# mLSTM heads 0 to 2: norm factors through a DRAM round trip in place of two diagonals and two products with ones

## The chip, the cores and the metric

The kernel runs on one core of a Trainium2 chip. The metric is the device time of one execution in microseconds (us), lower is better; a measurement is the median of several runs. The engines of the core have their own instruction streams and meet through semaphores: PE (matrix products; PEld is its weight load), DVE (vector), ACT (activation functions), POOL (here: memsets and the issue of some transfers) and SP (issue of the other transfers). Each engine takes its instructions strictly in the order of its own stream: an instruction that waits holds up everything behind it on that engine.

## The reference

The program is a two-layer encoder trunk on 512 tokens of width 1024: an mLSTM layer with a memory cross-attention beside it, a gated MLP, a band-attention layer, a second MLP. The change lies in the mLSTM layer, where each of four heads (192 wide) ends in a normalisation per token:

```python
num = einsum('bhts,bhse->bhte', s, vv) + inter[..., None] * einsum('bhtd,bhde->bhte', qq, c_st)
den = sum(s, axis=-1) + inter * einsum('bhtd,bhd->bht', qq, n_st)
h = num / maximum(abs(den), exp(-m_t))[..., None]
...
hm = hm * rsqrt(mean(hm * hm, axis=-1, keepdims=True) + EPS)      # per token and head
hm = hm.reshape(bsz, seq, A_WIDTH) * a_head_g
mix_out = hm * sigmoid(o)
...
x = x + concatenate([mix_out, mem_out], axis=-1) @ w_out
```

## The kernel before, in words

Activations lie with channels on the 128 partitions and the 512 tokens along a row. Numbers are kept to full precision by splitting each operand into a high and a low part (`split`: an ACT cast `L134` and a DVE subtraction `L135`), so that one product becomes three matmuls (`mm3`, lines 178 to 180). A weight block goes DRAM, `wr` (load on SP), `wh` (ACT cast), `wl` (DVE subtraction), with three buffers of each.

An mLSTM head (`mlstm_head(h)`) is a generator. It makes the causal scores of four blocks of 128 keys, each shorter than the one before (512, 384, 256, 128 queries): a row of decay terms (two small matmuls at lines 1134 and 1135), its exponential on ACT (`L1137`), the score product (three matmuls and two at `L517`), their product on DVE (`L1143`), and the split into the `pt` tile. Then `products(s)` multiplies the values with the four blocks of `pt`; block 3, 128 wide, comes last. Squares of the sums (`L1170`) are added over channels by products with a small constant (`mcf`, lines 1177 and 1178), which gives a column: one number per token, with tokens on partitions, 128 x 4. From this column DVE computes the factor `fc` per token with some 12 tiny instructions (`L1182` to `L232`).

`fc` has tokens on partitions, but is needed along the row and on all partitions. Before, `diagonal` (lines 134, 135, 241) split it into two parts and wrote each as four diagonal 128 x 128 blocks, and `spread` (`L254`) multiplied each of the two by a matrix of ones on PE. The sum, in PSUM, has the 512 factors along the row of every partition. `L1191` multiplies it with the head's output `og` (twice: 128 channels, and 64 that share a tile with another head), and the split of that result makes `mixes`, the operand of the output projection.

What stands beside the heads: `weave(job, fill, each)` runs a head's generator and takes, for each of its yields, `each` (or `each` times the number yielded) steps of one `mm3` from a queue of independent work, the projections that make later heads' queries, keys and gates (`a_tiles`, `a_memory_queries`). Head 0 is woven with the remaining projections, head 1 follows when `og[2]` is there, then memory attention over heads 0 and 1, head 2, memory attention over heads 2 and 3, and head 3 with the output projection:

```python
fill = chain(a_tiles(2), a_memory_queries(0), a_tiles(3, 4), a_tiles(5), a_memory_queries(1))
weave(mlstm_head(0), fill, 1.4)
until(lambda: og[2] is not None, fill)
weave(mlstm_head(1), fill, 1.125)
...
weave(mlstm_head(2), fill, 1.417)
```

The written order is not the last word: outside the stretches marked `manual_schedule` a scheduler puts each engine's instructions into a new order by its own estimate of when their inputs are there. `pin` keeps POOL's transfers in the order of the program. Memory attention, which follows heads 1 and 2, begins with queries (`head_queries`: memsets on POOL at `L497`, ACT `L498` and `L501`, DVE `L499`), scores (`L517`), a maximum (`L571`, DVE), an exponential (`L574`, ACT), a reciprocal and a scaling (`L575`, `L577`, DVE) and transposes on PE (`L586`).

Of the kernel before, what the change touches and what calls it, by code (L numbers as in the profile page):

```python
# [9 lines left out]
F32 = mybir.dt.float32  # L10
# [6 lines left out]
P = 128  # L17
D = 1024
S = 512
# [4 lines left out]
AH = 4  # L24
# [22 lines left out]
def f(ap):  # L47
    return ap.bitcast(F32)
# [3 lines left out]
def trunk(  # L52
# [19 lines left out]
    V, A, G = nc.vector, nc.scalar, nc.gpsimd  # L72
# [8 lines left out]
    dram = ctx.enter_context(tc.tile_pool(name="dram", bufs=1, space=bass.MemoryType.DRAM))  # L81

    def sb(tag, shape, dtype=F32):
        count[0] += 1
        return pool.tile(shape, dtype, tag=tag, name=f"{tag}{count[0]}", bufs=bufs[tag])

    def ps(tag):
        count[0] += 1
        return psum.tile([P, S], F32, tag=tag, name=f"p{tag}{count[0]}", bufs=pbufs[tag])

    def small(n=4):
        return sb("s", [P, 32])[:, :n]
# [38 lines left out]
    pin = tc.keep_in_program_order  # L131

    def split(hi, lo, src, on_act=True, pinned=False):
        high = A.copy(hi, src) if on_act else V.tensor_copy(hi, src)  # L134
        low = V.tensor_tensor(out=lo, in0=src, in1=f(hi), op=ALU.subtract)  # L135
        if pinned:
            pin(high)
            pin(low)
# [37 lines left out]
    def mm3(o, lh, ll, rh, rl, first, last, more=False):  # L176

        nc.tensor.matmul(o, lh, rh, start=first, stop=False, skip_group_check=more)  # L178
        nc.tensor.matmul(o, lh, rl, start=False, stop=False, skip_group_check=more)  # L179
        nc.tensor.matmul(o, ll, rh, start=False, stop=last, skip_group_check=more)  # L180

    def project(w, c0, act, tag="mm", lo=None):


        n = len(act)
        src = rows(w, c0, P)
        wh, wl = weights(src, n, P) if lo is None else summed_weights(lo, src, n, P)
        o = ps(tag)
        for k in range(n):
            mm3(o, wh[:, k, :], wl[:, k, :], act[k][0], act[k][1], k == 0, k == n - 1)  # L190
            yield
        return o
# [30 lines left out]
    def rsqrt(y, v):  # L223
        n = v.shape[-1]
        yi = y.bitcast(I32)
        V.tensor_scalar(yi, v.bitcast(I32), 1, None, op0=ALU.logical_shift_right)
        V.tensor_scalar(yi, yi, -1, 0x5F3759DF, op0=ALU.mult, op1=ALU.add)
        t = small(n)
        for _ in range(3):
            V.tensor_mul(t, y, y)  # L230
            V.scalar_tensor_tensor(t, t, -0.5, v, op0=ALU.mult, op1=ALU.mult)
            V.scalar_tensor_tensor(y, t, 1.5, y, op0=ALU.add, op1=ALU.mult)  # L232

    def diagonal(c):

        cs = [sb("s", [P, 32], F32R)[:, :TT] for _ in range(2)]
        split(*cs, c, on_act=False)
        dgs = []
        for c in cs:
            dg = sb("t", [P, S], F32R)  # L240
            V.tensor_tensor(
                out=dg.rearrange("p (a b) -> p a b", a=TT),
                in0=ident.unsqueeze(1).to_broadcast([P, TT, P]),
                in1=f(c).unsqueeze(2).to_broadcast([P, TT, P]),
                op=ALU.mult,
            )
            dgs.append(dg)
        return dgs

    def spread(dgs, tag):  # L250

        o = ps(tag)
        for i, dg in enumerate(dgs):
            nc.tensor.matmul(o, onesr, dg, start=i == 0, stop=i == 1)  # L254
        return o
# [255 lines left out]
    def head_scores(o, h, q, tsl, k, c, first, keys_first=False):  # L511

        for i, part in enumerate(q):
            a, b = part[h][:, tsl], k[h][:, c]
            if keys_first:
                a, b = b, a
            nc.tensor.matmul(o, a, b, start=first and i == 0, stop=i == 1)  # L517
# [24 lines left out]
    def queries(o, row):  # L542

        if row is None:
            return head_queries(o, HD**-0.5)
        q = sb("t", [P, S])
        V.scalar_tensor_tensor(q, o, HD**-0.5, row, op0=ALU.mult, op1=ALU.mult)
        return head_queries(q)
# [571 lines left out]
    def a_memory_queries(hp):  # L1120
        memq[hp] = queries((yield from project(w_in, 4 * AW + 2 * AH + hp * P, act)), None)

    def mlstm_head(h):
        hp, odd = divmod(h, 2)
        sh = 3 * hp + 1
        full = 3 * hp + 2 * odd
        rs = slice(HD, P) if odd else slice(0, HD)
        pt = sb("pt", [P, 5 * S], F32R)

        def weighted_scores(s):  # L1130
            n = S - s * P
            sl = slice(s * P, (s + 1) * P)
            r = ps("sc")
            nc.tensor.matmul(r[:, :n], sels[s % 2][:, h, :], rp[s // 2][:, s * P :], start=True, stop=False)
            nc.tensor.matmul(r[:, :P], identr, maskr, start=False, stop=True)
            e = sb("t", [P, S])
            A.activation(e[:, :n], r[:, :n], AF.Exp, bias=acol[:, s, h : h + 1])  # L1137
            yield
            o = ps("sc")
            kf, qf = ks[full], qs[full]  # L1140
            mm3(o[:, :n], kf[0][:, sl], kf[1][:, sl], qf[0][:, s * P :], qf[1][:, s * P :], True, False)
            head_scores(o[:, :n], odd, qs[sh], slice(s * P, S), ks[sh], sl, False, True)
            V.scalar_tensor_tensor(e[:, :n], o[:, :n], DH**-0.5, e[:, :n], op0=ALU.mult, op1=ALU.mult)  # L1143
            split(pt[:, RO[s] : RO[s + 1]], pt[:, 1280 + RO[s] : 1280 + RO[s + 1]], e[:, :n])
            yield

        nums = []

        def products(s):
            if not nums:  # L1150
                nums.extend(ps("tr") for _ in range(2))
            for o, c in zip(nums, (3 * P, 2 * P) if odd else (0, P)):
                mm3(
                    o[:, s * P :], vh[hp][s][:, c : c + P], vl[hp][s][:, c : c + P],
                    pt[:, RO[s] : RO[s + 1]], pt[:, 1280 + RO[s] : 1280 + RO[s + 1]], s == 0, s == TT - 1,
                )
            yield

        yield from weighted_scores(0)
        yield from weighted_scores(1)  # L1160
        yield from weighted_scores(2)
        yield from products(0)
        yield from weighted_scores(3)
        yield from products(1)
        yield from products(2)
        yield from products(3)
        sqs = []
        for o, j, r in ((nums[0], full, slice(0, P)), (nums[1], sh, rs)):
            sq = sb("t", [P, S])
            A.activation(sq, o, AF.Square)  # L1170
            sqs.append(sq)
            V.tensor_tensor(out=og[j][r, :], in0=o[r, :], in1=og[j][r, :], op=ALU.mult)
        yield
        st = ps("sc")
        for T in range(TT):
            sl = slice(T * P, (T + 1) * P)
            nc.tensor.matmul(st[:, 2 * T : 2 * T + 2], sqs[0][:, sl], mcf[:, 0, :], start=True, stop=False)
            nc.tensor.matmul(st[:, 2 * T : 2 * T + 2], sqs[1][:, sl], mcf[:, 1 + odd, :], start=False, stop=True)
            yield 0.581
        st = st[:, : 2 * TT].rearrange("p (t c) -> p t c", c=2)  # L1180
        z, fc = small(), small()
        V.tensor_tensor(out=z, in0=st[:, :, 1], in1=floor2[:, :, h], op=ALU.max)  # L1182
        V.tensor_scalar(z, z, EPS, 1e-35, op0=ALU.mult, op1=ALU.max)
        V.scalar_tensor_tensor(z, st[:, :, 0], 1.0 / DH, z, op0=ALU.mult, op1=ALU.add)
        rsqrt(fc, z)
        dg = diagonal(fc)
        yield 2.673
        fb = spread(dg, "sc")
        yield
        for j, r in ((full, slice(0, P)), (sh, rs)):  # L1190
            V.tensor_tensor(out=og[j][r, :], in0=fb[r, :], in1=og[j][r, :], op=ALU.mult)  # L1191
            if mixes[j] is None:
                mixes[j] = sb("u", [P, S], F32R), sb("u", [P, S], F32R)
            split(mixes[j][0][r, :], mixes[j][1][r, :], og[j][r, :])
# [10 lines left out]
    fill = chain(a_tiles(2), a_memory_queries(0), a_tiles(3, 4), a_tiles(5), a_memory_queries(1))  # L1205
    memkv = load_memory_kv(0)
# [3 lines that stand above are left out]
    until(lambda: memq[0] is not None, fill)  # L1210
    weave(memory_attention(memq[0], memkv, 0, mixes), fill, 1.463, 4)
    until(lambda: og[4] is not None, fill)
    weave(mlstm_head(2), fill, 1.417)
    run(fill)
    reload_x()
# [285 lines left out]
```

## Time and profile before

| | before |
|---|---|
| three timed runs | 1211.79, 1211.98, 1214.2 us; median 1211.98 us |
| profiled execution, first to last instruction (span) | 1209.9 us |
| PE busy | 1196.0 us, 99% of the span |
| DVE, ACT, POOL busy | 945.1, 711.1, 125.3 us |
| granted PE clock | 0.999 |
| last step of `fc` in heads 0, 1, 2 (`L232`) | starts at 135.76, 159.55, 216.91 us |

The profiled execution is known by its span; the median of the timed runs is 2.1 us above it, which lies ahead of the first and behind the last instruction or in the spread between runs. The three heads of the change lie between 130 and 225 us of the span. A row of the timeline gives start, length, engine, line and operation; matmuls are pipelined, so what one costs is the distance to the next start, not its length.

### The profile page before, as it was taken

The numbers are of one execution on the slowest core, as the hardware profiler recorded it, in microseconds if no ns is written. First come the engines' busy times: TensorE is split into PE (matmuls) and PEld (weight loads), VectorE is DVE, ScalarE is ACT, GpSimd is POOL, SyncE is SP. The second block draws the span as 40 slices with busy tenths as digits, with TensorE's granted clock in tenths as the row PEclk, the third lists the DMA queues.
The fourth block names the chain that finished last, engine by engine and source line by source line (L and its number), as shares of the span: only waits on it lengthen the run. The fifth ranks groups of instructions, "written<-read, shape, count | busy, mean of one in ns | idle before, by whom it ended". The sixth has DMA issues, their size and how long they took to land.

```text
span 1209.9 us, 18791 instructions
## 1 busy us (share of the span) xinstructions
PE 1196.0 (99%) x7063; PEld 1058.6 (87%) x7063; DVE 945.1 (78%) x1733; ACT 711.1 (59%) x1251; POOL 125.3 (10%) x197
## 2 busy tenths in 40 slices
PE   9999999999999999999999999999999999999997
PEld 9988888888889999999988888878889999999986
DVE  7878688877978777777698888997896777777755
ACT  4536577644655555555475667775565555555545
POOL 1300000001011111111011000001101001111100
PEclk9999999999999999999999999999999999999999
DMA  8634111347556676665563323145845466666551
GB/s 276 207 98 122 54 53 57 109 138 187 129 137 160 145 160 150 161 141 133 143 195 109 99 72 94 57 129 167 199 97 139 107 138 139 140 140 134 120 156 70
DMA packets 205260, 159.14 MB, mean 132 GB/s; under 512 B 7960, under 2 KB 185586, under 8 KB 205170
## 3 DMA queue, kind: packets, MB, share of 16 engines
q1 hardware_dynamic: 184338, 120.78, 34.1%
q0 software_dynamic: 20832, 37.17, 16.5%
q8 instruction: 55, 0.90, 0.3%
q14 instruction: 35, 0.29, 0.1%
HBM read 129.42 MB, written 32.44 MB: 134 GB/s over the span
## 4 chain that ended last, share of the span: by engine, by line
PE 94%; ACT 3%; DVE 2%; issue 0%; ACTq 0%; DVEq 0%
PE pmm L178 18%; PE pmm L180 18%; PE pmm L179 18%; PE ptr L178 6%; PE ptr L179 6%; PE ptr L180 6%; PE psc L180 5%; PE psc L178 5%; PE psc L179 5%; PE psc L517 2%; PE ptr L1328 1%; ACT wh L134 1%; PE ptr L1349 1%; PE ptr L1350 1%; PE ptr L586 0%; PE ptr L600 0%
## 5 line engine op out<-in xcount | busy, mean ns | idle before, releaser
L178 PE MATMUL pmm<-u,wh 128*128 128x512 f32 (+1 forms) x968 | 337.1, 349 | 0.1
L180 PE MATMUL pmm<-u,wl 128*128 128x512 f32 (+1 forms) x968 | 333.6, 345 | 0.0
L179 PE MATMUL pmm<-u,wh 128*128 128x512 f32 (+1 forms) x968 | 333.3, 345 | 0.1
L135 DVE TENSOR_TENSOR wl<-wr,wh 128x1024 fp32r<-128x1024 f32 (+4 forms) x168 | 194.7, 1160 | 96.7 <-ACT wh L134 96.0
L134 ACT CAST wh<-wr 128x1024 fp32r<-128x1024 f32 (+4 forms) x168 | 168.0, 1002 | 99.9 <-PE pmm L179 47.2
L180 PEld LDWEIGHTS pmm<-u,wl 128*128 128x128 f32 x968 | 183.6, 190 | 21.1
L179 PEld LDWEIGHTS pmm<-u,wh 128*128 128x128 f32 x968 | 183.9, 190 | 18.0 <-DVE u L135 0.8
L178 PEld LDWEIGHTS pmm<-u,wh 128*128 128x128 f32 x968 | 183.7, 190 | 17.7 <-ACT u L134 0.5
L178 PE MATMUL ptr<-u,wh 128*128 128x512 f32 x272 | 106.7, 392 | 0.0
L179 PE MATMUL ptr<-u,wh 128*128 128x512 f32 x272 | 106.5, 392 | 0.0
L180 PE MATMUL ptr<-u,wl 128*128 128x512 f32 x272 | 105.8, 389 | 0.0
L748 POOL DMA_DIRECT2D xspill<-t x64 | 56.0, 875 | 411.4 <-ACT t L747 408.6
L178 PE MATMUL pmm<-u,u 128*128 128x256 f32 x296 | 84.5, 285 | 2.5 <-ACT t L824 2.5
L180 PE MATMUL pmm<-u,u 128*128 128x256 f32 x296 | 84.0, 284 | 0.4 <-DVE u L135 0.4
L179 PE MATMUL pmm<-u,u 128*128 128x256 f32 x296 | 83.8, 283 | 0.0
L135 DVE TENSOR_TENSOR u<-pt,u 128x512 fp32r<-128x512 f32 x102 | 69.9, 688 | 9.7 <-ACT u L134 7.1
L178 PE MATMUL psc<-u,wh 128*128 128x256 f32 (+1 forms) x232 | 76.1, 328 | 0.0
L179 PE MATMUL psc<-u,wh 128*128 128x256 f32 (+1 forms) x232 | 75.9, 327 | 0.0
L747 ACT COPY t<-ptr 128x512 f32<-128x512 f32 x64 | 37.5, 586 | 65.3 <-PE ptr L180 65.3
L135 DVE TENSOR_TENSOR u<-t,u 128x512 fp32r<-128x512 f32 x78 | 53.4, 689 | 21.4 <-ACT u L134 21.1
L134 ACT CAST u<-pt 128x512 fp32r<-128x512 f32 x102 | 63.2, 619 | 11.4 <-DVE pt L859 11.1
L921 ACT ACTIVATE t<-t 128x512 f32<-128x512 f32 x34 | 21.6, 635 | 80.2 <-DVE t L657 80.2
(290 smaller groups left out, 2568.0 us busy)
## 6 DMA issues: line engine op xcount, KB each, us to landing
wr<-in_ffn_w_up_dram SPq DMA_DIRECT2D x54, 512.0 KB, 5.0
wr<-in_ffn_w_down_dram SPq DMA_DIRECT2D x38, 512.0 KB, 3.8
pt<-in_ffn_w_up_dram SPq DMA_DIRECT2D x34, 512.0 KB, 6.8
xspill<-t POOLq DMA_DIRECT2D x64, 256.0 KB, 4.8
wr<-in_a_w_in_dram SPq DMA_DIRECT2D x20, 512.0 KB, 3.8
xspill<-u POOLq DMA_DIRECT2D x32, 256.0 KB, 3.0
u<-xspill SPq DMA_DIRECT2D x32, 256.0 KB, 4.9
wr<-in_w_kv_dram SPq DMA_DIRECT2D x12, 512.0 KB, 4.1
```

The lines of the kernel that those rows point to most:

```text
L134: high = A.copy(hi, src) if on_act else V.tensor_copy(hi, src)
L135: low = V.tensor_tensor(out=lo, in0=src, in1=f(hi), op=ALU.subtract)
L178: nc.tensor.matmul(o, lh, rh, start=first, stop=False, skip_group_check=more)
L179: nc.tensor.matmul(o, lh, rl, start=False, stop=False, skip_group_check=more)
L180: nc.tensor.matmul(o, ll, rh, start=False, stop=last, skip_group_check=more)
L517: nc.tensor.matmul(o, a, b, start=first and i == 0, stop=i == 1)
L747: A.copy(t, o)
L748: G.dma_start(xspill[j], t, accum_op=ALU.add)
L921: A.activation(self.acc, self.acc, AF.Silu)
L1328: nc.tensor.transpose(tp[:, b * P : (b + 1) * P], es[T, h][:, b * P : (b + 1) * P], ident)
L1349: nc.tensor.matmul(o2[:, s * P :], w, hi_at(pts[h], s, s, TT - s), start=s == 0, stop=False)
L1350: nc.tensor.matmul(o2[:, s * P :], w, lo_at(pts[h], s, s, TT - s), start=False, stop=s == TT - 1)
```

## The change

For heads 0, 1 and 2 the factors go to a DRAM array `factors` (4 x 512) and come back: one POOL transfer writes `fc`, 128 partitions of 4 numbers, as 512 single numbers (token order), and a second one, which waits for the first, reads the 2 KB row into all 128 partitions of an SBUF tile with the tag `bias`. `L1191` then multiplies from that tile instead of from PSUM. The two splits, the two diagonals and the two matmuls of these heads are gone; head 3 keeps them. The two yields behind (2.673 and 1) become one of 3.1, so each of the three heads draws less other work at this place.

```diff
+    factors = dram.tile([AH, S], F32, name="factors")
+
     def mlstm_head(h):
...
         rsqrt(fc, z)
-        dg = diagonal(fc)
-        yield 2.673
-        fb = spread(dg, "sc")
-        yield
+        if h < AH - 1:
+            pin(G.dma_start(factors[h, :].rearrange("(t p) -> p t", p=P), fc))
+            fb = sb("bias", [P, S])
+            src = bass.AP(tensor=factors.tensor, offset=factors.offset + h * S, ap=[[0, P], [1, S]])
+            pin(G.dma_start(fb, src))
+            yield 3.1
+        else:
+            dg = diagonal(fc)
+            yield 2.673
+            fb = spread(dg, "sc")
+            yield
         for j, r in ((full, slice(0, P)), (sh, rs)):
             V.tensor_tensor(out=og[j][r, :], in0=fb[r, :], in1=og[j][r, :], op=ALU.mult)
```

Lines behind the new array stand 2 further down in the new kernel, and those from the multiplication on 9: `L1143` is `L1145` there, `L1182` is `L1184`, `L1191` is `L1200`. The scheduler also gives another order to PE, DVE and ACT from head 0 to the end of memory attention beside head 3; behind that the orders of all engines are the same, and SP's is the same throughout. Numbers behind a name are those of its buffer and differ between the two kernels for the same thing.

Head 0 on DVE, before: from the last step of `fc` on.

```order
L232 SCALAR_TENSOR_TENSOR s_1483<-s_1489,s_1483 128x4
L134 CAST s_1499<-s_1483 128x4
L135 TENSOR_TENSOR s_1500<-s_1483,s_1499 128x4
L241 TENSOR_TENSOR t_1503<-ident,s_1499 128x512
L241 TENSOR_TENSOR t_1505<-ident,s_1500 128x512
L1191 TENSOR_TENSOR u_1229<-psc_1529,u_1229 128x512
L1191 TENSOR_TENSOR u_1263<-psc_1529,u_1263 64x512
L1143 SCALAR_TENSOR_TENSOR t_1549<-psc_1554,t_1549 128x512
L135 TENSOR_TENSOR u_1537<-u_1229,u_1536 128x512
L1143 SCALAR_TENSOR_TENSOR t_1569<-psc_1574,t_1569 128x384
L135 TENSOR_TENSOR u_1542<-u_1263,u_1541 64x512
L135 TENSOR_TENSOR pt_1545<-t_1549,pt_1545 128x512
```

Head 0 on DVE, after: the same stretch, from the third score block (`t_1579`) to the low part of the fourth block of `pt`.

```order
L1145 SCALAR_TENSOR_TENSOR t_1579<-psc_1584,t_1579 128x256
L1200 TENSOR_TENSOR u_1230<-bias_1501,u_1230 128x512
L1200 TENSOR_TENSOR u_1264<-bias_1501,u_1264 64x512
L135 TENSOR_TENSOR pt_1535<-t_1579,pt_1535 128x256
L135 TENSOR_TENSOR u_1527<-u_1230,u_1526 128x512
L135 TENSOR_TENSOR u_1532<-u_1264,u_1531 64x512
L135 TENSOR_TENSOR wl_1779<-wr_1776,wh_1778 128x1024
L499 SCALAR_TENSOR_TENSOR u_1614<-pmm_1521,u_1612 64x512
L1145 SCALAR_TENSOR_TENSOR t_1610<-psc_1637,t_1610 128x128
L499 SCALAR_TENSOR_TENSOR u_1615<-pmm_1521,u_1613 64x512
L135 TENSOR_TENSOR pt_1535<-t_1610,pt_1535 128x128
```

The four instructions of `diagonal` are gone, and the multiplication by the factors, which stood ahead of the scores, now stands behind three of the four score blocks of head 1; behind it stand a weight split (`wl_1779`), the queries (`L499`) and the last block of `pt`.

POOL, after: the two transfers of each head and the memsets behind them; before, these memsets stood in a row with nothing between.

```order
L1189 DMA factors<-s_1484 128x4x1
L1192 DMA bias_1501<-factors 128x512
L497 MEMSET u_1614 64x512
L497 MEMSET u_1615 64x512
L1189 DMA factors<-s_1721 128x4x1
L1192 DMA bias_1738<-factors 128x512
L497 MEMSET u_1855 64x512
L497 MEMSET u_1856 64x512
L1189 DMA factors<-s_2248 128x4x1
L1192 DMA bias_2265<-factors 128x512
L497 MEMSET u_2319 64x512
L497 MEMSET u_2320 64x512
```

Each pair of memsets behind a head's transfers now follows the second one, which waits for the first to land. The pairs belong to the two memory queries (`u_1614`, `u_2319`) and to head 2's queries (`u_1855`).

Head 1 on ACT, before: from the casts of the head's result (`u_1771`, `u_1541`) to the exponentials of memory attention's first two tiles.

```order
L134 CAST u_1771<-u_1516 128x512
L134 CAST u_1541<-u_1263 64x512
L134 CAST wh_2025<-wr_2023 128x1024
L574 ACT_TABLE_LOAD
L574 ACTIVATE t_1828,s_1826<-psc_1809,s_1825 128x256
L1091 ACT_TABLE_LOAD
L1091 ACTIVATE t_1781<-t_1781 128x512
L574 ACT_TABLE_LOAD
L574 ACTIVATE t_1828,s_1826<-psc_1809,s_1825 128x256
L134 CAST u_1787<-t_1781 128x512
L574 ACTIVATE t_1843,s_1841<-psc_1810,s_1840 128x256 x2
```

The same place after, from the first half of the first exponential on.

```order
L574 ACTIVATE t_1807,s_1805<-psc_1788,s_1804 128x256
L1091 ACT_TABLE_LOAD
L1091 ACTIVATE t_1766<-t_1766 128x512
L134 CAST u_1750<-u_1512 128x512
L134 CAST u_1531<-u_1264 64x512
L134 CAST u_1772<-t_1766 128x512
L574 ACT_TABLE_LOAD
L574 ACTIVATE t_1807,s_1805<-psc_1788,s_1804 128x256
L574 ACTIVATE t_1822,s_1820<-psc_1789,s_1819 128x256 x2
```

The two casts (now `u_1750` and `u_1531`) stood ahead of all of these; now the first half of the first exponential and a Silu stand ahead of them, and the rest of the exponentials behind.

Head 2 on DVE, before: from the last step of `fc` to the queries of the memory attention that follows.

```order
L232 SCALAR_TENSOR_TENSOR s_2263<-s_2269,s_2263 128x4
L134 CAST s_2279<-s_2263 128x4
L135 TENSOR_TENSOR s_2280<-s_2263,s_2279 128x4
L241 TENSOR_TENSOR t_2283<-ident,s_2279 128x512
L241 TENSOR_TENSOR t_2285<-ident,s_2280 128x512
L1191 TENSOR_TENSOR u_2020<-psc_2309,u_2020 128x512
L1191 TENSOR_TENSOR u_2054<-psc_2309,u_2054 64x512
L135 TENSOR_TENSOR u_2317<-u_2020,u_2316 128x512
L135 TENSOR_TENSOR u_2322<-u_2054,u_2321 64x512
L135 TENSOR_TENSOR wl_2586<-wr_2583,wh_2585 128x384
L499 SCALAR_TENSOR_TENSOR u_2342<-pmm_2302,u_2340 64x512
L499 SCALAR_TENSOR_TENSOR u_2343<-pmm_2302,u_2341 64x512
```

The same place after, up to the first maximum of that memory attention.

```order
L232 SCALAR_TENSOR_TENSOR s_2248<-s_2254,s_2248 128x4
L135 TENSOR_TENSOR wl_2563<-wr_2560,wh_2562 128x384
L1200 TENSOR_TENSOR u_2005<-bias_2265,u_2005 128x512
L1200 TENSOR_TENSOR u_2039<-bias_2265,u_2039 64x512
L135 TENSOR_TENSOR u_2294<-u_2005,u_2293 128x512
L135 TENSOR_TENSOR u_2299<-u_2039,u_2298 64x512
L499 SCALAR_TENSOR_TENSOR u_2319<-pmm_2282,u_2317 64x512
L571 TENSOR_REDUCE s_2357<-psc_2347 128x2
```

The multiplication (`L1191`, now `L1200`) follows one small weight split behind the last step of `fc`; the queries of memory attention (`L499`), which its scores need, stay behind it. On PE the number of matmuls of 512 columns between two places changes with the order: between head 0's last `mcf` product and head 1's fourth block of `products` from 68 to 63, between head 1's last `mcf` product and the second transpose of memory attention from 86 to 71, and between head 2's last `mcf` product and the first scores of the next memory attention from 44 to 56.

## The prediction

> **What bounds the kernel now.** I read the page first (busy times, chain), then a table by stretches, then the timeline at the three heads, then the transfers.
>
> ```profile
> PE 1196.0 (99%) x7063; PEld 1058.6 (87%) x7063; DVE 945.1 (78%) x1733; ACT 711.1 (59%) x1251; POOL 125.3 (10%) x197
> ...
> PE 94%; ACT 3%; DVE 2%; issue 0%; ACTq 0%; DVEq 0%
> ```
>
> PE is busy 99% of 1209.9 us and makes up 94% of the chain that ended last; DVE, with 78%, has room as a whole. So time is won only where PE gets less to do, and lost where PE waits.
>
> ```profile
> sum 100.00, PE 99.90 PEld 83.90 DVE 78.10 ACT 68.77 POOL 2.08; mean PE 9.99 PEld 8.39 DVE 7.81 ACT 6.88 POOL 0.21
> ```
>
> This row sums ten stretches of 10 us, 130 to 230 us, which hold the change: PE is busy in 99.9 of 100.0 us. There is no idle PE time that a shorter chain could win back here; what the change gains is what its matmuls cost, and each microsecond that it makes PE wait is lost for good.
>
> **What it removes.** Six matmuls on PE (`L254`), each priced by the distance to the next start.
>
> ```profile
> 137.11 0.39 PE L254 MATMUL psc<-t,onesr 128*128 128x512 f32 x1
> 137.34 0.39 PE L1134 MATMUL psc<-u,sel 128*128 128x512 f32 x1
> ...
> 137.63 0.45 PE L254 MATMUL psc<-t,onesr 128*128 128x512 f32 x1
> 137.91 0.40 PE L178 MATMUL psc<-u,u 128*128 128x512 f32 x1
> ...
> 218.12 0.50 PE L254 MATMUL psc<-t,onesr 128*128 128x512 f32 x1
> 218.45 0.39 PE L178 MATMUL pmm<-u,wh 128*128 128x512 f32 x1
> 218.72 0.50 PE L254 MATMUL psc<-t,onesr 128*128 128x512 f32 x1
> 219.06 0.39 PE L179 MATMUL pmm<-u,wh 128*128 128x512 f32 x1
> ```
>
> Head 0: 0.23 + 0.28. Head 2: 0.33 + 0.34. For head 1 I take head 0's 0.51. Together 1.69: -1.7 us, and that is the whole gain. DVE loses four instructions a head; it is not the bound, and in the new order it waits at this very place, so that is worth nothing. The shorter yield only moves independent products to a later place: nothing by itself, but it changes when PE arrives where it must wait, which is counted below.
>
> **What it adds: L, the time from `fc` to the factors in SBUF.** It is two transfers in a row on POOL, each issued there; L decides everything. The nearest rows are a small and a large store from SBUF to DRAM, a read of 128 rows of 2 KB, and a transfer of 1024 pieces.
>
> ```profile
> L1237 POOL DMA_DIRECT2D rep<-maskf x12: 527/567/583, 356.0 to 515.8; - x12
> DMA to landing us min/median/max: 1.7/4.2/5.0
> ...
> L631 POOL DMA_DIRECT2D xspill<-u x16: 542/542/549, 262.4 to 849.6; - x16
> DMA to landing us min/median/max: 2.3/2.8/4.0
> ...
> L1303 POOL DMA_DIRECT2D bias<-rep x12: 538/538/748, 634.7 to 790.8; - x12
> DMA to landing us min/median/max: 2.9/3.1/4.7
> ...
> L169 POOL DMA_DIRECT2D pt<-in_ffn_w_up_dram x6: 1540/1566/1627, 290.5 to 881.4; - x6
> ```
>
> Store: a 16 KB store lands 1.7 to 5.0 us after its issue, a 256 KB one 2.3 to 4.0, median 2.8. `factors` is 8 KB, but in 512 pieces of 4 bytes. POOL needs 0.54 us to issue 128 pieces (`L1303`) and 1.57 for 1024 (`L169`), so 0.44 more for 512. I take 2.8 + 0.44 = 3.2; bounds 1.7 and 5.4. Read: 128 rows of 2 KB, 2.9 to 4.7; I take the median, 3.1. With 0.2 for two hand-overs, L is 6.5 us where the engines of the transfers are free, and 4.8 to 10.3 between the bounds. The Trainium skill ("DMA: Bandwidth & Descriptors", rules for kernel authors) says that a last dimension that isn't contiguous becomes one descriptor per element; here that is the store's 512 pieces. If instead each partition's four numbers went as one piece, the store would lose the 0.44, each wait below as much, and the sum would be +1.0 instead of +2.3. No row of the trace has 4-byte pieces, but more pieces do cost POOL more, so I keep the 0.44.
>
> ```profile
> 136.00:138.00 2.00, 2.00 (x11) 1.63 (x10) 1.49 (x4) 0.17 (x1) 0.00 (x0) 1.00 0.77 206
> ...
> 160.00:162.00 2.00, 2.00 (x11) 1.65 (x10) 2.00 (x4) 2.00 (x3) 0.00 (x0) 1.00 0.00 0
> ...
> 218.00:220.00 2.00, 2.00 (x9) 1.36 (x9) 1.41 (x4) 0.02 (x1) 0.00 (x0) 1.00 0.78 216
> ```
>
> The last two columns are the transfers' share and GB/s: the stores of heads 0 and 2 would meet a weight load (0.77 and 0.78 busy), head 1's none. I add 0.8 there, less than half the 2 us: L = 7.3, 6.5, 7.3. POOL itself is free when `fc` comes; its memsets behind the read go out some 4 us later than `fc`, before anyone needs them: nothing. SP's order doesn't change: nothing.
>
> **Who waits for L.** The result of a head is needed by the output projection only, long after. But DVE and ACT work in order: `L1200` (`L1191` before) waits at the head of DVE's queue, the casts of its result at the head of ACT's, and behind them stands what PE needs next.
>
> ```profile
> 135.76 0.16 DVE L232 SCALAR_TENSOR_TENSOR s<-s,s 128x4 f32<-128x4 f32 x1
> 138.11 1.28 DVE L1191 TENSOR_TENSOR u<-psc,u 128x512 f32<-128x512 f32 x2 [0.59 <-PE psc L254]
> ...
> 142.44 1.05 ACT L134 CAST wh<-wr 128x1024 fp32r<-128x1024 f32 x1
> 143.40 0.58 ACT L498 ACTIVATE u<-pmm 64x512 fp32r<-64x512 f32 x1
> 144.30 0.62 ACT L501 CAST u<-u 64x512 fp32r<-64x512 f32 x1
> 144.95 0.37 ACT L1137 ACTIVATE t<-psc,acol 128x128 f32<-128x128 f32 x1
> ...
> 147.73 0.29 DVE L135 TENSOR_TENSOR pt<-t,pt 128x128 fp32r<-128x128 f32 x1 [0.37 <-ACT pt L134]
> ...
> 150.55 0.22 PE L178 MATMUL ptr<-pt,u 128*128 128x128 f32 x1
> ```
>
> *Head 0.* `fc` is there at 135.92. PE comes to the fourth block of `products` at 150.55 before; with 5 matmuls fewer ahead of it, the two of `L254` among them (0.23 each), at 149.35. It needs the last part of `pt`. In the new order this is, counted from the landing: first multiplication and its cast 0.7 + 0.7, second cast 0.65 (both 1.28 on DVE), weight cast 1.06, the exponential 0.4, `L498` 0.58 and `L501` 0.62, a second `L498` 0.6 between the two `L499`, the second `L499` 0.65 and the last subtraction 0.3: 6.6 us. PE waits 135.92 + L + 6.6 - 149.35 = L - 6.8: 0.5 us.
>
> ```profile
> 153.64 1.23 DVE L135 TENSOR_TENSOR wl<-wr,wh 128x1024 fp32r<-128x1024 f32 x1 [0.56 <-ACT wh L134]
> ...
> 155.87 0.17 DVE L1182 TENSOR_TENSOR s<-psc,floor 128x4 f32<-128x4 f32 x1 [0.22 <-PE psc L1178]
> 159.55 0.16 DVE L232 SCALAR_TENSOR_TENSOR s<-s,s 128x4 f32<-128x4 f32 x1
> ...
> 163.69 1.35 ACT L134 CAST u<-u 128x512 fp32r<-128x512 f32 x2 [1.56 <-DVE u L1191]
> 171.65 1.28 ACT L574 ACT_TABLE_LOAD   x1
> ...
> 176.31 0.60 DVE L577 TENSOR_SCALAR t<-t,s 128x256 f32<-128x256 f32 x2
> ...
> 177.77 0.60 PE L586 MATMUL ptr<-ident,t 128*128 128x128 f32 x4
> ```
>
> *Head 1.* Let S be the end of its last `mcf` product, 155.83 before (`L1182` starts 0.04 later). `fc` ends at 159.71 before, S + 3.9; a weight split (the first row, 1.23, 1.15 of it not overlapped) and one more step of the convolution, as wide as a multiplication of 512 (0.65), now stand ahead of it: S + 5.7. PE reaches the second transpose of memory attention (`L586`) at 177.77, S + 21.9; with 15 matmuls fewer ahead (3.4), at S + 18.5. From the landing to its input: first multiplication 0.7, the two casts 1.35, and then what before ran from the table load at 171.65 to the end of the scaling at 176.91, 5.3, with one convolution step less between (0.65): 6.7 us. PE waits S + 5.7 + L + 6.7 - (S + 18.5) = L - 6.1: 0.4 us.
>
> ```profile
> 216.91 0.16 DVE L232 SCALAR_TENSOR_TENSOR s<-s,s 128x4 f32<-128x4 f32 x1
> ...
> 219.26 1.28 DVE L1191 TENSOR_TENSOR u<-psc,u 128x512 f32<-128x512 f32 x2 [0.59 <-PE psc L254]
> ...
> 222.39 0.68 DVE L499 SCALAR_TENSOR_TENSOR u<-pmm,u 64x512 fp32r<-64x512 f32 x1
> ...
> 222.94 0.28 PE L517 MATMUL psc<-u,u 128*128 128x256 f32 x1
> ```
>
> *Head 2* has the least cover. `fc` ends at 217.07, the scores `L517` start at 222.94; with 14 other matmuls (3.2) in the place of the two of `L254` (0.7), at 225.4. Before, the queries `L499` ended 3.8 us after `L1191` started, with a weight cast of 384 columns between (0.4, by the 1.05 of 1024 columns) that now stands ahead: 3.4. PE waits 217.07 + L + 3.4 - 225.4 = L - 4.9: 2.4 us. Behind that, the exponentials and scalings of this memory attention run in a new order. Below, 0: before, PE waits for none of them. Above, 1.3: the table load of the exponentials (1.28 in the row at 171.65) stands whole behind the late queries. Nothing tells which, so I take the middle, 0.7.
>
> **The sum**: -1.7 + 0.5 + 0.4 + 2.4 + 0.7 = +2.3, on the profiled span of 1209.9. The store of single numbers is the one term without a row of its kind, and its error is the likelier on the long side (0.1 us more in L costs 0.3 in the sum), so I go a little up, to +2.7; on the median of the runs, 1211.98, which stands 2.1 above the span, **1214.7 us**. About 0.2% (2.4 us) is what a measurement of this kernel can tell from no change, so this lies at that edge.
>
> **Rivals.**
> *A, the forecast:* L between 6.5 and 8.5. At 6.5 in every head the waits are 0, 0.4, 1.6 and 0.7: +1.0, 1213.0. At 8.5: 1.7 + 2.4 + 3.6 + 0.7 - 1.7 = +6.7, 1218.7. Chance 0.53.
> *B, not slower:* the round trip is hidden. It needs both transfers near their shortest rows, 1.7 to 2.3 and 2.9; from L = 4.9 downward no head waits, and the time is 1211.98 - 1.7 = 1210.3, with L = 5.9 and half of the 0.7 1211.6. For it speaks that the transfers are idle in part of this stretch (0.00 at 160 to 162); against it, that it takes the minimum of both rows at once, three times. The Trainium skill ("DMA: Bandwidth & Descriptors", anatomy of one DMA) gives 2.0 us plus bytes over 436 GB/s per transfer: an estimate from that page of 2.0 + 2.6 = 4.6 us, and so this rival. The trace's rows, 2.8 and 3.1, are longer than that. Chance 0.27, and within it 0.05 that it comes out faster by over 2.4 us.
> *C, much slower:* 512 single writes into the same few rows of DRAM are slow, or a weight load holds the read back; L = 8.5 to 10.3. At 10.3: 3.5 + 4.2 + 5.4 + 1.3 - 1.7 = +12.7, 1224.7. For it: the 16 KB store's median of 4.2, though it is the smaller one; against it: the 256 KB store's 2.8, and a read of 3.1 in the median. Chance 0.13.
> *D:* the new order removes a wait that I don't see, or `L254` cost more than its distance; faster by 2 to 4 us, 1209. Against it: 99.9 of 100.0 us busy. Chance 0.07.
>
> **Numbers.** Faster: 0.05 of B and 0.06 of D: 0.11. Same: the rest of B, 0.22, and of A what lies below +2.4, 0.19, and 0.01 of D: 0.42. Slower: the rest of A, 0.34, and C: 0.47. The range reaches from B's 1210.2 to 1220.0, in the lower part of C; A alone spans 1213.0 to 1218.7.
>
> **What would show it.** In the changed profile: PE busy less by about 2 us and idle time on PE in 130 to 235 that was not there; DVE idle ahead of `L1200`, ended by the transfer into `bias`, longest at head 2; PE's `L517` behind head 2 waiting for `L499`, its `products` at head 0 for `pt`. The landing times of `factors` and `bias` give L itself. If L is under 6 or PE shows no new idle time, the forecast is wrong and B holds; if L is right and PE does not wait, my walk through ACT's and DVE's new order is what failed.

## The result: 2.9% slower, and the profile after

| | before | after |
|---|---|---|
| median of the timed runs, on one chip | 1212.42 us (4 runs, 1211.79 to 1214.20) | 1247.59 us (4 runs, 1245.48 to 1250.52) |
| ratio | | 1.029 (95% interval 1.0273 to 1.0306), +35.2 us |
| profiled execution: span | 1209.9 us | 1245.8 us |

The forecast was 1214.7 us, its range ended at 1220.0. The busy times on the page of the changed kernel:

```profile
PE 1201.3 (96%) x7057; PEld 1061.8 (85%) x7057; DVE 941.0 (76%) x1721; ACT 710.1 (57%) x1251; POOL 129.3 (10%) x203
```

Read this against the span first. PE is idle for 1245.8 - 1201.3 = 44.5 us, where it was 13.9 before: 30.6 us more. But its busy time has also risen, by 5.3 us, though six matmuls are gone, worth 1.7 by the prediction. So some 7.0 us are the same matmuls taking longer. 30.6 + 5.3 is the whole difference of the spans, 35.9.

The round trip itself, on DVE and POOL. `L232` is the last step of `fc`, `L1189` the store, `L1192` the read, `L1200` the multiplication that waits for it (the bracket gives the idle time before it and what ended that):

```profile
136.89 0.16 DVE L232 SCALAR_TENSOR_TENSOR s<-s,s 128x4 f32<-128x4 f32 x1
137.34 0.76 POOL L1189 DMA_DIRECT2D factors<-s  x1 [87.68 <-DVE s L232]
147.14 0.54 POOL L1192 DMA_DIRECT2D bias<-factors  x1 [9.04 <-DMA factors<-s]
151.28 1.28 DVE L1200 TENSOR_TENSOR u<-bias,u 128x512 f32<-128x512 f32 x2 [8.79 <-DMA bias<-factors]
...
170.08 0.16 DVE L232 SCALAR_TENSOR_TENSOR s<-s,s 128x4 f32<-128x4 f32 x1
170.54 0.76 POOL L1189 DMA_DIRECT2D factors<-s  x1 [21.72 <-DVE s L232]
180.68 0.54 POOL L1192 DMA_DIRECT2D bias<-factors  x1 [9.38 <-DMA factors<-s]
186.83 1.41 DVE L1200 TENSOR_TENSOR u<-bias,u 128x512 f32<-128x512 f32 x2 [10.94 <-DMA bias<-factors]
...
238.02 0.16 DVE L232 SCALAR_TENSOR_TENSOR s<-s,s 128x4 f32<-128x4 f32 x1
238.47 0.76 POOL L1189 DMA_DIRECT2D factors<-s  x1 [56.12 <-DVE s L232]
249.28 0.54 POOL L1192 DMA_DIRECT2D bias<-factors  x1 [10.05 <-DMA factors<-s]
256.35 1.28 DVE L1200 TENSOR_TENSOR u<-bias,u 128x512 f32<-128x512 f32 x2 [14.07 <-DMA bias<-factors]
```

| | head 0 | head 1 | head 2 |
|---|---|---|---|
| store: from its issue to the read's issue | 9.8 | 10.1 | 10.8 |
| read: from its issue to `L1200` | 4.1 | 6.2 | 7.1 |
| L, from the end of `L232` to `L1200` | 14.2 | 16.6 | 18.2 |
| L in the prediction | 7.3 | 6.5 | 7.3 |

Who waited, 120 to 290 us (total, times, longest):

```profile
PE psc L517 <- ACT u L501: 12.9, 1, 12.9
...
PE psc L517 <- ACT t L574: 9.8, 1, 9.8
...
PE ptr L179 <- DVE pt L135: 3.8, 2, 3.5
...
PE ptr L178 <- ACT pt L134: 2.5, 1, 2.5
```

PE waits 12.9 us behind head 2 (scores, for the late queries), 9.8 beside head 1's memory attention and some 6 at head 0 (the `pt` blocks): 29 us, nearly the whole 30.6. And this is PE behind the second of these waits, with two rows of a later time for comparison:

```profile
181.32 0.39 PE L179 MATMUL pmm<-u,wh 128*128 128x512 f32 x1
191.46 1.22 PE L517 MATMUL psc<-u,u 128*128 128x256 f32 x4 [9.76 <-ACT t L574]
192.48 0.63 PE L180 MATMUL pmm<-u,wl 128*128 128x512 f32 x1
192.91 0.63 PE L178 MATMUL pmm<-u,wh 128*128 128x512 f32 x1
...
196.35 0.39 PE L178 MATMUL pmm<-u,wh 128*128 128x512 f32 x1
196.57 0.39 PE L179 MATMUL pmm<-u,wh 128*128 128x512 f32 x1
```

A 128x512 product takes 0.43 us from start to start at 192.48 and 0.22 at 196.35: for about 4 us behind the wait PE runs at half speed. The table of 10 us windows (last columns: granted clock, share and GB/s of the transfers) has the same:

```profile
190.00:200.00 10.00, 8.54 (x38) 7.25 (x39) 7.73 (x21) 8.84 (x21) 0.00 (x0) 0.73 0.01 2
...
240.00:250.00 10.00, 6.57 (x29) 5.09 (x28) 0.56 (x1) 0.52 (x1) 0.69 (x2) 1.00 0.80 34
250.00:260.00 10.00, 0.52 (x2) 0.49 (x3) 3.17 (x5) 2.60 (x5) 0.89 (x2) 0.50 0.72 251
```

The Trainium skill ("TensorE: Matmul & The Clock Gate", Part 1) says that PE falls to half clock after an idle window of about 3.4 us and needs about 3.4 us of work to come back; that agrees with the 9.8 us of waiting and the 4 us at 0.43. Not every run here fits it so simply: shorter waits brought the half speed too, and in three runs it lasted longer (last section).

### The profile page after: what moved, and what is told of

Its sections match the earlier page's. It is cut to its first block, busy times and chain, and to the rows that moved or that the text cites. A ratio compares the mean times of both kernels' runs of the same rounds, so it can differ in the third digit from the quotient of the medians.

```text
span 1245.8 us, 18779 instructions
## 1 busy us (share of the span) xinstructions
PE 1201.3 (96%) x7057; PEld 1061.8 (85%) x7057; DVE 941.0 (76%) x1721; ACT 710.1 (57%) x1251; POOL 129.3 (10%) x203
## 4 chain that ended last, share of the span: by engine, by line
PE 76%; issue 14%; DVE 3%; ACT 3%; DMA 2%; POOL 1%; SPq 0%; POOLq 0%; DVEq 0%; ACTq 0%
PE pmm L178 14%; PE pmm L180 13%; PE pmm L179 13%; PE ptr L179 5%; PE ptr L178 5%; PE ptr L180 5%; PE psc L178 5%; PE psc L180 5%; PE psc L179 5%; PE psc L517 2%; PE ptr L1337 1%; DMA bias<-factors 1%; DMA factors<-s 1%; PE ptr L1358 1%; PE ptr L1359 1%
## 5 line engine op out<-in xcount | busy, mean ns | idle before, releaser
L179 PEld LDWEIGHTS pmm<-u,wh 128*128 128x128 f32 x968 | 184.5, 191 | 18.4 <-DVE u L135 0.8
```

## The experiments

Theory: the store of 512 single numbers is what failed, and all else follows (DVE waits, ACT and PE wait behind it, PE's clock drops). Rivals: a fixed cost of any store that is read back, the read, the way POOL issues it, and the new order itself. The experiments are numbered in the order in which they ran, and told by subject. Where times of the store are given, they go from its issue to the read's issue, heads 0, 1 and 2.

**Experiment 1, pieces of 16 bytes.** The four numbers of a partition go out as one piece, and the multiplication reads the row with a step:

```diff
-            pin(G.dma_start(factors[h, :].rearrange("(t p) -> p t", p=P), fc))
+            pin(G.dma_start(factors[h, :].rearrange("(p t) -> p t", t=TT), fc))
...
-            V.tensor_tensor(out=og[j][r, :], in0=fb[r, :], in1=og[j][r, :], op=ALU.mult)
+                o = o.rearrange("c (t p) -> c t p", t=TT)
+                V.tensor_tensor(out=o, in0=fb[r, :].rearrange("c (p t) -> c t p", t=TT), in1=o, op=ALU.mult)
```

> The store writes the four numbers of a partition as one piece of 16 bytes: 128 pieces in place of 512, the same 2 KB of DRAM. The multiplication reads the row with a step of four numbers, so the result is the same. Theory P (the store's time goes with its number of pieces, over a floor of about 2.5 us, as the 256 KB store's shortest landing): 2.5 + (9.6 - 2.5)/4 = 4.3 us from issue to landing; L falls by 5.3 in each head, to about 9, 11 and 13, and the median from 1247.6 to 1224 to 1232. Rival F (a fixed time for a store that a read has to wait for, whatever its pieces): the store still lands after 9 to 10 us, 1245 to 1250. Rival R (the read of one 2 KB row by 128 partitions is the slow part): the store was never late by itself, the read still takes 4 to 7 us; does not by itself say that the store gets shorter.

Measured: 1217.87 us beside 1211.59, ratio 1.0044 (1.0027 to 1.0060). The store takes 3.8, 2.2 and 3.0 us. Head 1 on POOL, store and read:

```profile
165.08 0.54 POOL L1189 DMA_DIRECT2D factors<-s  x1 [20.25 <-DVE s L232]
167.30 0.54 POOL L1192 DMA_DIRECT2D bias<-factors  x1 [1.68 <-DMA factors<-s]
```

F falls: no store has a fixed 9 us. The store is shorter than P's 4.3 too, so its time does not simply go with the number of pieces. The read, too, is back at 3.5 to 4.3 us, so the 6.2 and 7.1 us of the changed kernel are not its own price; what held it up there was not tested.

**Experiment 2, four pieces of 512 bytes.** PE transposes the column, DVE copies it, and four rows are stored:

```diff
+            tp = ps("sc")
+            nc.tensor.transpose(tp[:TT, :P], fc, ident)
+            row = sb("t", [P, S])[:TT, :P]
+            V.tensor_copy(row, tp[:TT, :P])
+            pin(G.dma_start(factors[h, :].rearrange("(t p) -> t p", p=P), row))
```

> The column is transposed on PE (128 x 4 to 4 x 128), copied to SBUF by DVE and stored as four rows of 512 bytes. Theory P: the store lands after 2 to 3 us; with about 1.0 us for transpose and copy L falls by 6, to 8, 10 and 12 us; 1221 to 1230. Rival F: the store still takes 9 to 10 us, L is longer by the transpose and copy, 1248 to 1253.

Measured: 1216.07 us, ratio 1.0034 (1.0021 to 1.0047); store 3.0, 2.1 and 2.9 us, as P had it. The time lies below P's range, since the reads too got shorter. With 4 pieces the store is hardly faster than with 128 pieces of 16 bytes.

**Experiment 3, 512 pieces far apart.** This is the changed store, only each number goes 512 bytes from the next:

```diff
-    factors = dram.tile([AH, S], F32, name="factors")
+    factors = dram.tile([AH, S, P], F32, name="factors")
...
+            pin(G.dma_start(factors[h, :, 0].rearrange("(t p) -> p t", p=P), fc))
```

> As the changed kernel, 512 pieces of 4 bytes, but each piece goes 512 bytes from the next, so that no two lie in the same 512 bytes of DRAM. The row that is read back holds four of the factors and ones, so the factors of these heads are left out of the output. Theory P (each piece costs its time, wherever it goes): store 9 to 10.5 us, 1245 to 1250. Rival N (pieces in the same few bytes of DRAM hold each other up): the store lands after 3 to 5 us, 1218 to 1232.

Measured: 1218.36 us, ratio 1.0054 (1.0039 to 1.0069).

```profile
162.89 0.76 POOL L1191 DMA_DIRECT2D factors<-s  x1 [19.59 <-DVE s L232]
165.39 0.54 POOL L1194 DMA_DIRECT2D bias<-factors  x1 [1.74 <-DMA factors<-s]
```

As many pieces of the same 4 bytes take 3.8, 2.5 and 3.5 us instead of 9.8 to 10.8: N, and P is out. POOL's issue, 0.76 us, is as long as in the changed kernel; what differs is only where in DRAM the pieces land.

Four further looks, of one run each, narrow this down.

Experiment 6, 64 bytes from one to the next (`factors = dram.tile([AH, S, 16], ...)`):

> As the changed kernel, 512 pieces of 4 bytes, each 64 bytes from the next in DRAM (512 bytes apart the store took 2.5 to 3.8 us, side by side 9.8 to 10.8). The row read back holds 32 of the factors and ones. If pieces hold each other up within 64 bytes: 2.5 to 4 us from the store's issue to the read's, about 1218 us in all. If within 512 bytes: 4 us or more, towards 10; 1225 to 1247.

Measured: 3.8, 2.5 and 3.7 us, 1219.04 us in all. As at 512 bytes.

Experiment 7, side by side, but the four numbers of one partition as neighbours (the 16-byte order above, with a gap behind each number in SBUF, so that each goes as a piece of its own):

> 512 pieces of 4 bytes again, side by side in DRAM, but in the order of the first experiment: the four numbers of a partition are neighbours, and the order is put right in the multiplication. The column is kept with a gap behind each number, so that each stays a piece of its own. In the changed kernel the neighbours in DRAM come from neighbouring partitions. If pieces side by side are slow whoever writes them: the store takes 9 to 11 us as in the changed kernel, 1240 to 1250. If it matters from which partition the neighbours come: 2.5 to 5 us, 1217 to 1225.

Measured: 8.6, 9.2 and 10.6 us; 1243.70 us. Slow whoever writes the neighbour.

Experiment 12, one column only, 128 pieces side by side in 512 bytes (`factors[h, :P].unsqueeze(1), fc[:, 0:1]`):

> As the changed kernel, but only the first of the four columns is stored: 128 pieces of 4 bytes side by side in 512 bytes of DRAM; the rest of the row holds ones, so three quarters of the factors are left out. If the time goes with the number of pieces in all: 2.5 + 7/4, about 4.3 us from the store's issue to the read's. If it is set by how many pieces share one small stretch of DRAM (as many here as in each stretch of the changed kernel): 9 to 10 us as there.

Measured: 8.6, 7.4 and 8.9 us; 1245.96 us.

```profile
138.03 0.54 POOL L1191 DMA_DIRECT2D factors<-s  x1 [87.26 <-DVE s L232]
146.63 0.54 POOL L1194 DMA_DIRECT2D bias<-factors  x1 [8.06 <-DMA factors<-s]
```

A quarter of the pieces, nearly the same time: what counts is that 4-byte pieces lie side by side in DRAM, not how many there are in all. How few neighbours are enough was not tried.

Experiment 8, SP issues the store (`nc.sync.dma_start` for `G.dma_start`):

> As the changed kernel, but SP issues the store in place of POOL (the read stays on POOL); weight loads behind it on SP wait for the factors. If the pieces themselves are slow: 9 to 11 us from the store's issue to the read's, and 1245 us or more. If POOL's way of issuing them is slow: 2 to 4 us, 1216 to 1225, and more where a weight load now comes late.

Measured: 1244.93 us. SP issues at 136.76, 172.30 and 236.79, and POOL's reads follow 10.0, 8.9 and 10.5 us later: the pieces are slow, not POOL.

**Experiment 4, the same transfers and nobody waiting.** The store stays at 512 numbers; the multiplication stands later:

```diff
+        def finish():
+            for j, r in ((full, slice(0, P)), (sh, rs)):
+                pin(V.tensor_tensor(out=og[j][r, :], in0=fb[r, :], in1=og[j][r, :], op=ALU.mult))
...
     weave(mlstm_head(1), fill, 1.125)
     until(lambda: memq[0] is not None, fill)
+    late.pop(0)()
     weave(memory_attention(memq[0], memkv, 0, mixes), fill, 1.463, 4)
+    late.pop(0)()
...
+    weave(islice(job, 8), fill, 0.475)
+    late.pop(0)()
```

> The transfers stay as in the changed kernel, but nobody needs them soon: the multiplication by the factors and its casts stand some 30 us later for heads 0 and 1 and some 18 us later for head 2, and head 2's read is issued behind the memsets of the memory queries. Theory W (all of the loss is PE waiting behind the late multiplication, and the slow clock after those waits): 35 us come back, the windows of 120 to 250 us show PE busy as before, and what is left is the 1.7 us of the six matmuls: 1210 to 1212. Rival T (the transfers themselves hold up other transfers, such as weight loads, or the new order costs by itself): 1216 or more.

Measured: 1216.94 us, ratio 1.0041 (1.0026 to 1.0056): some 30 of the 35 us are back with the slow store still in place, which then took 8 to 9 us, so the loss was the waiting and what followed from it. But it is neither W's 1210 to 1212 nor a proof of T: DVE waited once more, at head 2, and PE behind it.

```profile
233.73 0.69 DVE L1205 TENSOR_TENSOR u<-bias,u 128x512 f32<-128x512 f32 x1 [3.71 <-DMA bias<-factors]
...
235.08 3.27 PE L600 MATMUL ptr<-pt,u 128*128 128x512 f32 x8 [3.61 <-DVE pt L135]
```

Head 2's cover of 18 us was too short for its round trip. Experiment 5, both cures together, decides between W and T:

> Both cures at once: the store in 128 pieces of 16 bytes (as in the first experiment) and the multiplication some 30 us later for heads 0 and 1 and some 18 us later for head 2 (as in the fourth). Theory W (the late version still lost time only because head 2's factors came 3.7 us after DVE wanted them): now they come before, PE waits nowhere in 130 to 250 us, and the 1.7 us of the six matmuls are won: 1209.5 to 1211 beside 1211.6. Rival T (the later multiplication or the transfers cost by themselves, beside heads that do not wait): still 1214 or more, with the loss in the window of 230 to 240 us.

Measured: 1211.20 us beside 1211.77, ratio 0.9997 (0.9988 to 1.0006). Heads 0 and 1 no longer cost anything and T falls, but the 1.7 us are not won either. PE still lost 0.4 us at one place, where its products stand behind head 2's multiplication on DVE (0.61 us from start to start, where 0.22 is the rule):

```profile
231.54 0.40 PE L179 MATMUL pmm<-u,wh 128*128 128x512 f32 x1
232.15 2.10 PE L600 MATMUL ptr<-pt,u 128*128 128x512 f32 x8 [0.21 <-DVE pt L135]
```

So experiment 11 lets head 2's multiplication follow the last sum of the memory attention (`then()` behind `mixes[6 + hp] = values(outs)`):

> As the fifth experiment, with head 2's multiplication a little later still, behind the last sum of the memory attention, so that its two instructions no longer stand between the scalings and the last parts of `pt` that PE's products (L600) waited for. If those waits (0.4 and 0.2 us at 231.5 and 232.2) and the order around them are what kept the fifth from winning the 1.7 us: 1209.5 to 1210.7 beside 1211.7. If the six matmuls cost PE less than the distance to the next start said: 1211 to 1212 again.

Measured: 1210.85 us beside 1211.91, ratio 0.9991 (0.9982 to 0.9999). This is the one version that beats the kernel before as well, by 1.1 us, at the edge of what can be told, and it lies between the two ranges that were expected. Its interval overlaps that of experiment 5, so that the last move won anything is not shown. PE's busy time, and the ten windows from 130 to 230 us:

```profile
PE 1195.1 (99%) x7057; PEld 1058.4 (88%) x7057; DVE 942.1 (78%) x1721; ACT 707.6 (59%) x1249; POOL 128.7 (11%) x203
...
sum 100.00, PE 100.00 PEld 84.03 DVE 74.18 ACT 66.72 POOL 5.85; mean PE 10.00 PEld 8.40 DVE 7.42 ACT 6.67 POOL 0.58
```

PE waits nowhere in this stretch, and has 0.9 us less to do than before (1196.0).

**Experiments 9 and 10, the clock.** An attempt to keep PE's clock up through the two long waits, beside a repeat of the changed kernel:

```diff
+        def idle_products(n):
+            o = ps("mm")
+            for _ in range(n):
+                pin(nc.tensor.matmul(o, onesr, acts[0][0], start=True, stop=True))
...
+            if early and (hp, T2) in ((0, 1), (1, 0)):
+                idle_products(48 if hp else 32)
```

> The changed kernel once more, as the yardstick for the next one on the same chip: 1245 to 1250 by every theory.

> The changed kernel with products put into PE's two long waits: 32 ahead of the score products that waited 9.8 us (memory attention beside head 1) and 48 ahead of those that waited 12.9 us (behind head 2), each 0.23 us, their sum read by nobody. 2.5 and 2 us of each wait are left. Nothing that PE waits for gets sooner. Theory C (beside the 29 us of idle PE some 6 us of the loss are PE at a lower granted clock behind its long waits, 4.8 of them behind these two): the windows behind them show a clock of 1.00, the time falls by 4 to 5 us, to 1242 to 1244. Rival (the lower clock in the windows is only an average over idle time, and PE's work behind the waits is not slower): no change, or up to 1 us longer.

Measured: the repeat 1243.70 us beside 1211.91, ratio 1.0264 (1.0250 to 1.0278), somewhat less than the first time and just under the 1245 to 1250 expected, with stores of 9.0, 9.9 and 8.7 us; with the products 1256.84, ratio 1.0366 (1.0350 to 1.0382), 13 us longer, where 4 to 5 us shorter or no change was expected. The edit did not do what it was to do. The scheduler moved some 5 us of projections from ahead of each wait to behind it: beside head 1, PE had reached the wait 11.0 us after the store's issue in the repeat, and now reached the idle products after 5.6 (170.95 to 176.51). So 6.0 and 5.2 us of waiting were left instead of 2.5 and 2:

```profile
176.51 7.65 PE L566 MATMUL pmm<-u,onesr 128*128 128x512 f32 x32
...
190.38 0.80 PE L517 MATMUL psc<-u,u 128*128 128x256 f32 x2 [5.98 <-ACT t L581]
190.97 0.63 PE L178 MATMUL pmm<-u,wh 128*128 128x512 f32 x1
191.40 0.63 PE L179 MATMUL pmm<-u,wh 128*128 128x512 f32 x1
```

PE's busy time, in the repeat and with the products:

```profile
PE 1203.2 (97%) x7057; PEld 1063.8 (86%) x7057; DVE 940.8 (76%) x1721; ACT 710.9 (57%) x1251; POOL 129.3 (10%) x203
```

```profile
PE 1225.9 (98%) x7137; PEld 1082.6 (86%) x7137; DVE 941.4 (75%) x1721; ACT 711.5 (57%) x1251; POOL 129.3 (10%) x203
```

That is 22.7 us more of busy PE (80 products of 0.23 are 18.4); with spans of 1242.0 and 1256.2 it is 38.8 and 30.3 us of idle PE, 8.5 less; 14.2 longer in all. The 4.3 us beyond the 18.4 need not come from the products. Already behind head 0's waits, ahead of the first of them, PE ran at half speed from 151 to 168 us, in the repeat only from 157 to 161. The window of 160 to 170 us, with PE busy throughout in both, shows it in the number of matmuls and in the granted clock (third column from the right), the repeat first:

```profile
160.00:170.00 10.00, 10.00 (x54) 8.65 (x53) 5.38 (x19) 4.47 (x6) 0.49 (x1) 0.96 0.19 53
```

```profile
160.00:170.00 10.00, 10.00 (x33) 8.40 (x34) 4.68 (x15) 3.02 (x4) 0.00 (x0) 0.58 0.19 53
```

As a test of what the clock costs it decides nothing by its time. Its rows do refute the rival: behind a wait of 6.0 us the products stand 0.43 apart, so the work is slower and the low clock is not an average over idle time.

## Why the prediction was wrong, step by step

*The step that failed is L*, and in it the store. The prediction took 2.8 + 0.44 = 3.2 us, bounded by 1.7 and 5.4 from the rows of larger stores, and said that no row had 4-byte pieces. (The 8 KB that it gives for `factors` is the whole array; one store moves 2 KB.) The 0.44 for POOL's issue was in the right direction, though only 0.22 came of it (0.76 us against 0.54). The rest was not: 9.8 to 10.8 us, nearly twice the upper bound. The bound assumed that a store of small pieces is at worst as slow as a store of larger ones. The experiments put the excess of some 7 us down to 4-byte pieces side by side: 64 bytes apart, the same 512 pieces took 2.5 to 3.8, which is what the prediction had taken. Rival C named this mechanism, "512 single writes into the same few rows of DRAM are slow", with 0.13, but priced it by the same bound, so that L ended at 10.3 and the range at 1220.

The rule that the prediction weighed, of the Trainium skill ("DMA: Bandwidth & Descriptors", rules for kernel authors: a last dimension that isn't contiguous becomes one descriptor per element), bore more than was drawn from it: avoiding the single numbers was put at 0.44 us a head, and is worth about 7. But it speaks of the number of pieces, and experiments 3 and 12 show that this is not what cost the time.

*The read* was taken as 3.1, 3.9 where it meets a weight load. In the changed kernel it took 4.1, 6.2 and 7.1. With 16-byte pieces, 3.5 to 4.3: the median row was a fair choice, and most of the surplus is gone where the store is quick.

*The walk from L to PE's waits* held. With the measured L its formulas give 14.2 - 6.8 = 7.4, 16.6 - 6.1 = 10.5 and 18.2 - 4.9 = 13.3; measured were about 6.3, 9.8 and 12.9. (The terms listed for head 0 add up to 6.3 us and not 6.6, so its formula should have been L - 7.1, which gives 7.1.) Head 2 is where the prediction put it (`L517` behind the queries; what came last was ACT's `L501`, not DVE's `L499`). At head 0 PE stopped first for the third block of `pt`, which the walk had not looked at, then for the fourth. At head 1 the wait stood not at the transposes (`L586`) but earlier, at the scores `L517`, which need a PSUM buffer that a late exponential still held. With pieces 512 bytes apart, L at head 2 was 8.9 us (218.97 to 227.56, and 0.3 for the hand-over), so 4.0 of waiting; PE waited 3.6:

```profile
230.69 1.32 PE L517 MATMUL psc<-u,u 128*128 128x256 f32 x4 [3.61 <-ACT u L501]
231.81 0.63 PE L180 MATMUL pmm<-u,wl 128*128 128x512 f32 x1
232.24 0.63 PE L178 MATMUL pmm<-u,wh 128*128 128x512 f32 x1
```

*What the sum did not have* is the clock. These rows show it as well: 3.6 us of waiting are followed by products 0.43 apart. With the measured L the sum comes to -1.7 + 31.2 + 0.7 = 30.2, the spans differ by 35.9, and the 7.0 us by which PE's own work grew stand beside measured waits that were 2 shorter than the formulas. That the work is slower is shown by its spacing. In the changed kernel's trace PE works at this spacing from 157.0 to 161.1, 191.5 to 195.3 and 259.5 to 263.4 us, some 12 us in all, which at half speed cost some 6 of the 7.0. No run took this away by itself, since experiment 10 failed to.

*The gain*, -1.7 for six matmuls, could be seen only in experiment 11: 1.1 us in the median (interval 0.1 to 2.2), 0.9 in PE's busy time. So 1.7 is not excluded, but the distance to the next start may be somewhat too high a price.

*Head 2's remainder*, 0.7 for the new order behind it, cannot be told apart from the rest. *POOL's memsets and SP*, costed at nothing: no wait of PE was for them.

*The signs that were named* came as listed except one: PE busy did not fall by 2 us, it rose by 5.3, which was the clock.

## What to carry to other kernels

Before a column goes through DRAM, look at where its pieces land: single numbers side by side cost 7 us more than the same numbers 64 bytes apart or in pieces of 16 bytes, and putting the order right in the instruction that reads them back costs far less (1.09 us instead of 0.69 on DVE). Ask of a new wait what stands behind it on its engine, then shorten the wait and move the waiting instruction back: here each of the two alone gave some 30 of the 35 us (experiments 1 and 4), and only both together all of it (5 and 11). And where PE comes to wait for a few microseconds, add what its work behind the wait costs at half speed, here as a rule for some 4 to 6 us.

## What the hardware showed that was not expected

- 4-byte pieces side by side in DRAM: 7.4 to 11.2 us from the store's issue to that of a read behind it, in 512 pieces or 128, from POOL or from SP; 64 or 512 bytes apart: 2.5 to 3.8; 16 bytes side by side: 2.2 to 3.9; 512 bytes: 2.1 to 3.0. The Trainium skill ("DMA: Bandwidth & Descriptors", Specifications) states that below 512 bytes a transfer is a read-modify-write; that alone does not cost the time, since pieces of 4 bytes far apart and of 16 bytes side by side are below 512 as well. What exactly holds neighbours up stays open: if they simply went one behind the other, 16-byte pieces, a quarter as many in a stretch, should lose a quarter of the 7 us, 1.8; they lose 0.1 to 0.8 against the 512-byte rows.
- Such a store holds up others. From 240 to 250 us the transfers were busy for a share of 0.80 and moved 34 GB/s (the window above), and the 128 KB weight blocks between 120 and 290 us landed 9.6 us after their issue, with 16-byte pieces 3.4 (median, the two rows below, of the changed kernel and of experiment 1). Of such blocks issued from 216 to 228 us, beside head 2's store, six landed after 8.3 us (median) in experiment 4 and 3.8 in experiment 3; before the change, without a store, it was 2.8. That it did PE no harm, since PE was waiting anyway, is argued and not shown.

```profile
wr<-in_a_w_out_dram SPq DMA_DIRECT2D x8, 128.0 KB, 9.6
```

```profile
wr<-in_a_w_out_dram SPq DMA_DIRECT2D x8, 128.0 KB, 3.4
```

- A multiplication on DVE that reads one operand with a step of four numbers takes 1.09 us for 128x512 (experiment 11); without the step one takes 0.68 to 0.69, and two together, the second on 64 partitions, 1.28 (the changed kernel, the row at 256.35).

```profile
160.47 1.09 DVE L1209 TENSOR_TENSOR u<-bias,u 128x512 f32<-128x512 f32 x1
```

- PE's half speed did not need one long wait. In experiment 2 two waits of 0.8 and 1.2 us, shortly behind each other, were enough:

```profile
227.44 0.50 PE L178 MATMUL pmm<-u,wh 128*128 128x512 f32 x1 [0.79 <-ACT u L134]
229.18 1.12 PE L517 MATMUL psc<-u,u 128*128 128x256 f32 x4 [1.23 <-ACT u L501]
230.09 0.63 PE L179 MATMUL pmm<-u,wh 128*128 128x512 f32 x1
230.52 0.63 PE L180 MATMUL pmm<-u,wl 128*128 128x512 f32 x1
```

  Nor did it always end after 4 to 6 us of work: behind head 0's waits it went on to 168 us in experiment 10 and to 170 in experiments 8 and 12, some 14 us behind the last of these waits, although PE was busy all the while from 160 us on. At head 0 of the changed kernel, on the other hand, the products right behind the wait of 3.5 us (153.7 to 154.1) still stand 0.23 apart, and only those behind the second wait (2.5 us) are slow. What decides it is not shown here.
